# Rows beyond 128 of an expert as float32 strips on unsplit weights, and an earlier gather at expert 0

## The chip, the core and the metric

The kernel runs on one core of a Trainium2 chip. The metric is device time in microseconds (us) of one execution; three runs of the kernel before gave 1434.61 to 1436.72 us, median 1436.69. Engines are named as the profile names them: PE is TensorE's matmul, PEld its weight load, DVE VectorE, ACT ScalarE, POOL GpSimd, SP SyncE, which here issues the loads of weights.

## What is computed

A two-layer model on 512 tokens of width 1024 in float32: one layer of attention with a feed-forward block, one of a short convolution with a mixture of experts. The change is in the mixture: every token goes to 2 of 8 experts, and each expert is a gated block of inner width 1408.

```python
D_MODEL, SEQ, N_EXPERTS, TOP_K, D_FF_EXPERT = 1024, 512, 8, 2, 1408

def moe_swiglu(x, w_router, b_router, w_gate, w_up, w_down):
    ...
    logits = (xt @ w_router).astype(jnp.float32) + b_router.astype(jnp.float32)
    top_logit, top_e = lax.top_k(logits, TOP_K)
    top_w = jax.nn.softmax(top_logit, axis=-1)
    ...
        h = jax.nn.silu(xb @ w_gate[e]) * (xb @ w_up[e])
        return (h @ w_down[e]) * w[:, None].astype(h.dtype)
    ...
    y = jnp.zeros((T, D), x.dtype).at[tok_buf].add(out.reshape(n_rows, D).astype(x.dtype))
```

With the inputs used, the eight experts get 107, 120, 139, 126, 116, 133, 149 and 134 rows (counted from the reference's own inputs): experts 2, 5, 6 and 7 have more than 128.

## The kernel before

Everything ahead of the experts is the same in both kernels and is left aside; in the profiled execution the experts run from 892 us to the end.

**Precision.** A float32 product is made of two parts. `split` writes a number's high part in TensorE's float32r format with ACT (a cast) and the remainder with DVE (a subtraction); `mm3` (lines 502 to 505) then adds three matmuls: high by high, high by low, low by high. This holds for the rows, which are the stationary operand, and for the weights, which stream past.

**Weights.** Class `Weights` keeps one list of all weight chunks in the order of use. A chunk is up to 128 x 1024 float32 (512 KB). `pump` issues a load on SP's queue for the next chunk whenever a raw room is free, and splits a loaded chunk (line 351 on ACT, line 352 on DVE) into a split part whenever a part room is free, up to the number of pieces it is given. A raw room is free again as soon as the chunk is split; a part room when `done` is called for the piece. By `weight_room` there are 6 raw and 3 part rooms in `wb`, 4 and 5 in `wc`, 3 parts in `wa`: 10 raw, 11 parts. Pools `wb` and `wc` are filled in during the layers before; `wc` only begins ahead of expert 0 (line 1662).

**An expert.** `prep` transposes 128 gathered rows into `xgT` (high and low). `gate_up(e, j)` does one of three column groups (512, 512, 384): for u = 0 (gate) and u = 1 (up) 8 steps of `mm3` over the width of 1024, one 512-KB chunk for two steps, 4 chunks for each half. Silu goes to ACT, the product `h` to DVE. `h_transposes` turns `h` into `hT`. `down(e, c)` makes one 512-column half of the output in 11 steps with 6 chunks; the rows are scaled with their share by ACT, and POOL scatters them, adding to the output in DRAM. `done` is called behind each group for all its chunks.

**The rest.** Rows 129 to 192 of an expert (XT = 64) are gathered and transposed as `xe`, high and low side by side as one stationary tile of 128 columns. Behind each group's main matmuls a branch on the expert's row count (`tc.If`, line 1793 in `gate_up`, line 1846 in `down`) runs the block for the rest: per step one matmul of the 128-wide tile on the weights' high part and one of its first 64 columns on their low part (`extra`, lines 1756 to 1761), 32 for the two halves of a group and 22 for a half of down. `both` adds the two lots of 64 result rows (ACT copy at line 1753, DVE addition at line 1754). Down has such a block for each of its halves. A last block (`most > 128 + XT`), which no expert here needs, handles any further rows.

**Order.** The engines run in the order in which the code issues. At expert 0, `first_between` runs between the gate and the up half of the first group: the slot matmuls (line 1685) and the index (line 1687), the gather of the rest's rows (line 1721 on POOL), the shares (lines 1694 to 1704), and the loading of the row counts into registers (line 1710). Then come the up half, the transposes of the rest (line 1745) and the branch.

Of the kernel before, what the change touches and what calls it, by code (L numbers as in the profile page):

```python
# [13 lines left out]
F32 = mybir.dt.float32  # L14
# [24 lines left out]
XT = 64  # L39
# [263 lines left out]
class Weights:  # L303
# [13 lines left out]
    def add(self, src, offset, *shapes):  # L317

        m = sum(k * n for k, n in shapes)
        at = 0  # L320
        for k, n in shapes:
            self.add_part(src, offset, m, at, k, n)
            at += k * n
        return offset + 128 * m

    def add_part(self, src, offset, row, at, k, n):

        self.pieces.append(Piece(len(self.chunks), 0, k, n, True))
        self.chunks.append((bass.AP(tensor=src.tensor, offset=src.offset + offset + at, ap=[[row, 128], [1, k * n]]), k * n))

    def pump(self, pieces=99):

        while True:
# [7 lines left out]
            elif (pieces and self.ready < len(self.pieces) and self.pieces[self.ready].chunk in self.raw  # L341
# [11 lines left out]
                if p.last:  # L353
# [16 lines left out]

    def resume(self, chunks, ahead):
# [7 lines left out]
class Piece:  # L379
    def __init__(self, chunk, at, k, n, last):  # L380
        self.chunk, self.at, self.k, self.n, self.last = chunk, at, k, n, last
# [4 lines left out]
    def lo(self, k, cols=slice(None)):  # L386
        return self.t[:, 1, k * self.n:(k + 1) * self.n][:, cols]

# [28 lines left out]
def kernel(ctx: ExitStack, tc: tile.TileContext, A, out, stop=None):  # L417
# [71 lines left out]
    for e in range(E):  # L489
        off = e * ng  # L490
        for _, n in MOE_GROUPS:
            for a in ("w_eg", "w_eu"):
                W.add(A[a], off, (2, n), (2, n))
                W.add(A[a], off + 128 * 4 * n, (2, n), (2, n))
            off += 128 * 8 * n
        off = e * nd
        for c in range(2):
            for _, n in DN_BLOCKS:
                off = W.add(A["w_ed"], off, (2, 512), (n - 2, 512))
# [1177 lines left out]
    def slots(e):  # L1677
# [10 lines left out]
        yield  # L1688

# [23 lines left out]
    with ExitStack() as l0:  # L1713
# [26 lines left out]
        def extra_prep(e):  # L1740
            xe = mo.tile([128, KD, 2 * XT], F32R, name="xe")
# [4 lines left out]
            split(xe[:, :, :XT], xe[:, :, XT:], pt)  # L1746
            S["e", e] = xe

        def both(dst, p):

            n = dst.shape[1]
            t = mo.tile([XT, 512], F32, name="tb")
            ACT.copy(t[:, :n], p[XT:])  # L1753
            DVE.tensor_tensor(dst, p[:XT], t[:, :n], op=OP.add)

        def extra(p, xh2, wh, wl, start, stop):
            if start:
                PE.matmul(p, xh2, wh, start=True, stop=False)
            PE.matmul(p[:XT], xh2[:, :XT], wl, start=False, stop=False)
            if not start:  # L1760
                PE.matmul(p, xh2, wh, start=False, stop=stop)

        def gate_up(e, j, between=None, after=None):
            c0, n = MOE_GROUPS[j]
            cs = slice(c0, c0 + n)
            if j == 0:
                S["h", e] = mo.tile([128, FE], F32, name="h"), mo.tile([XT, FE], F32, name="he")
                S["hTe", e] = mo.tile([128, NFE, 2 * XT], F32R, name="hTe")
# [3 lines left out]
            ge = mo.tile([XT, 512], F32, name="ge")  # L1772
            ws = [], []
# [221 lines left out]
```

## Time and profile before

| | us |
|---|---|
| median of three runs | 1436.69 |
| lowest and highest run | 1434.61, 1436.72 |
| profiled execution, its own time | 1433.92 |
| its span in the trace | 1432.2 |
| of that, the experts (892.53 to the end) | 539.7 |
| mean granted TensorE clock, of full speed | 0.993 |

The profile is one execution. Its page gives busy time by engine over the whole span; windows of the trace give the same for a stretch; the timeline lists instructions, each with its start, its length, and in brackets how long its engine was idle before it and what ended that. Matmuls are pipelined: the length of one is longer than the time from its start to the next one's start, and it is the latter that adds up. DMA share is the mean busy share of the core's 16 DMA engines. A granted clock of 1.00 is 2.4 GHz, 0.50 is 1.2 GHz.

### The profile page before, as it was taken

The numbers are of one execution on the slowest core, as the hardware profiler recorded it, in microseconds if no ns is written. First come the engines' busy times: TensorE is split into PE (matmuls) and PEld (weight loads), VectorE is DVE, ScalarE is ACT, GpSimd is POOL, SyncE is SP. The second block draws the span as 40 slices with busy tenths as digits, with TensorE's granted clock in tenths as the row PEclk, the third lists the DMA queues.
The fourth block names the chain that finished last, engine by engine and source line by source line (L and its number), as shares of the span: only waits on it lengthen the run. The fifth ranks groups of instructions, "written<-read, shape, count | busy, mean of one in ns | idle before, by whom it ended". The sixth has DMA issues, their size and how long they took to land. (4 is left out here: it accounts for less than half of the span.)

```text
span 1432.2 us, 19340 instructions
## 1 busy us (share of the span) xinstructions
PE 1393.0 (97%) x6956; PEld 1136.0 (79%) x6957; DVE 857.3 (60%) x1391; ACT 700.7 (49%) x1168; POOL 204.4 (14%) x308
## 2 busy tenths in 40 slices
PE   7998999999999999999999999899999999999997
PEld 6866778879888888888988888778788787878785
DVE  4358897855433333434554445899677996666563
ACT  4545896834222221322422223677466775655553
POOL 2258553410000000000000000201102012011100
PEclk9999999999999999999999999999999999999999
DMA  5243001034232232313332224899778997767751
GB/s 190 83 143 122 16 16 60 30 133 148 90 102 89 89 103 74 118 59 118 100 107 94 97 89 167 261 386 378 272 244 282 376 376 269 255 205 245 259 195 24
DMA packets 69416, 231.42 MB, mean 162 GB/s; under 512 B 8752, under 2 KB 10044, under 8 KB 69308
## 3 DMA queue, kind: packets, MB, share of 16 engines
q1 hardware_dynamic: 64332, 217.39, 44.1%
q0 software_dynamic: 3632, 11.06, 3.3%
q10 hardware_dynamic: 1344, 1.58, 0.3%
q8 instruction: 62, 1.02, 0.3%
q14 instruction: 46, 0.38, 0.1%
HBM read 220.53 MB, written 9.47 MB: 161 GB/s over the span
## 5 line engine op out<-in xcount | busy, mean ns | idle before, releaser
L352 DVE TENSOR_TENSOR wbp<-wbr,wbp 128x1024 fp32r<-128x1024 f32 (+2 forms) x104 | 120.9, 1177 | 141.9 <-ACT wbp L351 140.5
L351 ACT CAST wbp<-wbr 128x1024 fp32r<-128x1024 f32 (+2 forms) x104 | 103.8, 1015 | 199.2 <-PE pg L505 108.2
L352 DVE TENSOR_TENSOR wap<-wbr,wap 128x1024 fp32r<-128x1024 f32 (+2 forms) x98 | 113.5, 1173 | 96.0 <-ACT wap L351 94.7
L351 ACT CAST wap<-wbr 128x1024 fp32r<-128x1024 f32 (+2 forms) x98 | 97.8, 1013 | 110.6 <-PE pg L505 73.3
L514 POOL TENSOR_TENSOR rs<-rs,mhalf 128x1 f32<-128x1 f32 x11 | 6.1, 551 | 566.4 <-DVE rs L513 566.4
L352 DVE TENSOR_TENSOR wcp<-wbr,wcp 128x1024 fp32r<-128x1024 f32 (+2 forms) x73 | 80.1, 1128 | 6.0 <-ACT wcp L351 5.0
L1753 ACT COPY tb<-pg 64x512 f32<-64x512 f32 (+1 forms) x32 | 17.8, 556 | 117.5 <-issue 94.8
L351 ACT CAST wcp<-wbr 128x1024 fp32r<-128x1024 f32 (+2 forms) x73 | 68.6, 978 | 9.2 <-PEq L1793 7.7
L503 PE MATMUL pg<-wcp,xgTh 128*128 128x512 f32 (+1 forms) x174 | 66.2, 381 | 0.9 <-PEq L1793 0.2
L505 PE MATMUL pg<-wcp,xgTl 128*128 128x512 f32 (+1 forms) x174 | 65.0, 374 | 0.0
L504 PE MATMUL pg<-wcp,xgTh 128*128 128x512 f32 (+1 forms) x174 | 65.0, 374 | 0.0
L352 DVE TENSOR_TENSOR wcp<-wcr,wcp 128x1024 fp32r<-128x1024 f32 (+2 forms) x57 | 62.5, 1123 | 4.1 <-ACT wcp L351 2.3
L1845 POOL DMA_INDIRECT out_dram<-y,idx x8 | 16.9, 2107 | 291.3 <-ACT y L1840 291.3
L351 ACT CAST wcp<-wcr 128x1024 fp32r<-128x1024 f32 (+2 forms) x57 | 53.6, 972 | 5.0 <-PEq L1793 4.8
L1424 DVE TENSOR_TENSOR x<-pd,x 128x512 f32<-128x512 f32 x48 | 32.3, 688 | 39.2 <-PE pd L505 39.1
L602 POOL TENSOR_TENSOR s<-s,mhalf 128x4 f32<-128x4 f32 (+4 forms) x37 | 35.7, 974 | 69.2 <-DVE s L601 54.7
L1721 POOL DMA_INDIRECT xg<-xd,idx x15 | 20.5, 1364 | 153.5 <-DVE idx L1687 127.9
L626 DVE TENSOR_TENSOR wap<-r,wap 128x1024 fp32r<-128x1024 f32 (+3 forms) x24 | 26.3, 1095 | 26.5 <-ACT wap L623 26.4
L503 PE MATMUL pg<-wbp,xgTh 128*128 128x512 f32 (+1 forms) x104 | 39.4, 379 | 2.3 <-ACT wcp L351 1.7
L503 PE MATMUL pd<-wap,hT 128*128 128x512 f32 x104 | 41.2, 396 | 0.0
L505 PE MATMUL pd<-wap,hT 128*128 128x512 f32 x104 | 41.1, 395 | 0.0
L504 PE MATMUL pd<-wap,hT 128*128 128x512 f32 x104 | 41.1, 395 | 0.0
(561 smaller groups left out, 4235.5 us busy)
## 6 DMA issues: line engine op xcount, KB each, us to landing
wbr<-w_ed SPq DMA_DIRECT2D x48, 512.0 KB, 7.6
wbr<-w_gu SPq DMA_DIRECT2D x44, 512.0 KB, 3.7
wbr<-w_eg SPq DMA_DIRECT2D x40, 512.0 KB, 7.2
wbr<-w_eu SPq DMA_DIRECT2D x40, 512.0 KB, 7.6
wcr<-w_ed SPq DMA_DIRECT2D x32, 512.0 KB, 7.1
wbr<-w_od_in SPq DMA_DIRECT2D x24, 512.0 KB, 3.7
wcr<-w_eg SPq DMA_DIRECT2D x24, 512.0 KB, 7.3
wcr<-w_eu SPq DMA_DIRECT2D x24, 512.0 KB, 7.8
```

The source lines that it names most:

```text
L351: self.nc.scalar.copy(p.t[:, 0, :m], src)
L352: self.nc.vector.tensor_tensor(p.t[:, 1, :m], src, p.t[:, 0, :m].bitcast(F32), op=OP.subtract)
L503: PE.matmul(o, lh, rh, start=start, stop=False)
L504: PE.matmul(o, lh, rl, start=False, stop=False)
L505: PE.matmul(o, ll, rh, start=False, stop=stop)
L514: POOL.tensor_tensor(dst, dst, mhalf[:p, :m], op=OP.pow)
L602: op("POOL", 70 + 78 * n, lambda: POOL.tensor_tensor(rs(), rs(), mhalf[:rs().shape[0], :n], op=OP.pow), (), [buf])
L626: op("DVE", m, lambda: DVE.tensor_tensor(p.t[:, 1, :m], src(), p.t[:, 0, :m].bitcast(F32), op=OP.subtract), [raw], [part])
L1424: DVE.tensor_tensor(x[i][:, cs], ps[c], x[i][:, cs], op=OP.add)
L1721: POOL.indirect_dma_start(out=t, out_offset=None, in_=src, in_offset=rows_of(e, b, n))
L1753: ACT.copy(t[:, :n], p[XT:])
L1845: POOL.indirect_dma_start(out=out, out_offset=rows_of(e, 0), in_=y, in_offset=None, compute_op=OP.add)
```

## The change

XT becomes 32. Rows 129 to 160 of an expert are multiplied in plain float32 on the weights as they were loaded. `xe` and `hTe` hold one float32 copy, 32 columns wide. `strips` puts each 32-column stationary tile on one of four column positions of TensorE's array: step k with operand u goes to result rows 64 (k mod 2) + 32 u, so gate and up of a group (or both halves of down) run in one block, in one PSUM bank, and even and odd steps add up on strips of their own. `halves_of` and one DVE addition join the even and the odd lot; the row's share is multiplied into `he` rather than into `ye`. Down's first half has no branch any more; its second does both halves.

For that, raw chunks are kept (`keep=True`) until `let_go`, behind the group's strips, or behind both halves of down. Split parts are released piece by piece as `mm3` is done with them. The rooms shift: `wc` has 13 raw and 1 part in place of 4 and 5, which makes 19 raw and 7 parts in all. At expert 0, four pieces in place of two are split ahead of the first rows, the second half of the rows is split behind the slots' one-hot rows, and `first_early` runs the slot matmuls and issues the gather behind step 3 of the gate half.

```diff
-XT = 64
+XT = 32
...
-                if p.last:
+                if p.keep:
+                    p.raw, p.raw_slot = self.raw.pop(p.chunk)
+                else:
                     self.raw_free.append(self.raw.pop(p.chunk)[1])
...
+    def let_go(self, *pieces):
+
+        self.raw_free += [p.raw_slot for p in pieces]
+        self.pump(0)
...
+    def whole(self, k):
+        return self.raw[:, k * self.n:(k + 1) * self.n]
...
-    W.pump(2)
-    for b, pt in enumerate(pts):
-        split(first_T[0][:, 4 * b:4 * b + 4], first_T[1][:, 4 * b:4 * b + 4], pt)
-    lx.close()
-    weight_room("wc", 4, 5)
-    W.pump(0)
+    W.pump(4)
+    first_split = lambda b: split(first_T[0][:, 4 * b:4 * b + 4], first_T[1][:, 4 * b:4 * b + 4], pts[b])
+    first_split(0)
...
+    first_slots = slots(0)
+    next(first_slots)
+    first_split(1)
+    lx.close()
+    weight_room("wc", 13, 1)
+    W.pump(1)
...
+        def strips(p, rows, weights):
+
+
+
+            n = len(rows)
+            for k, (x_, pair) in enumerate(zip(rows, weights)):
+                for u, w in enumerate(pair):
+                    o = 64 * (k % 2) + 32 * u
+                    PE.matmul(p[o:o + 32], x_, w, start=k < 2, stop=k >= n - 2)
...
                     mm3(p, xgh[:, k], xgl[:, k], w.hi(k % 2), w.lo(k % 2), k == 0, k == KD - 1)
+                    if k % 2:
+                        W.done(w, splits=0)
                     if k == 3:
+                        if early and u == 0:
+                            early()
                         W.pump(GATE_UP_PACE[2 + u])
...
             with tc.If(regs[e] > 128):
-                for u in range(2):
-                    p = psB.tile([128, 512], F32, name="pg", tag="g")[:, :n]
-                    for k in range(KD):
-                        w = ws[u][k // 2]
-                        extra(p, xe[:, k], w.hi(k % 2), w.lo(k % 2), k == 0, k == KD - 1)
-                    if u == 0:
-                        both(ge[:, :n], p)
-                        ACT.activation(ge[:, :n], ge[:, :n], AF.Silu)
-                    else:
-                        both(he[:, cs], p)
-                        DVE.tensor_tensor(he[:, cs], he[:, cs], ge[:, :n], op=OP.mult)
+                p = psB.tile([128, 512], F32, name="pg", tag="g")[:, :n]
+                strips(p, [xe[:, k] for k in range(KD)],
+                       [[ws[u][k // 2].whole(k % 2) for u in (1, 0)] for k in range(KD)])
+                DVE.tensor_tensor(su[:, :n], p[:64], halves_of(p, n), op=OP.add)
+                ACT.activation(ge[:, :n], su[32:, :n], AF.Silu)
+                DVE.scalar_tensor_tensor(he[:, cs], su[:32, :n], S["w", e, 1][:, e:e + 1], ge[:, :n], op0=OP.mult,
+                                         op1=OP.mult)
...
-            W.done(*ws[0], *ws[1], splits=GATE_UP_PACE[1])
+            W.let_go(*ws[0], *ws[1])
+            W.pump(GATE_UP_PACE[1])
...
+            if c == 0:
+                return
...
+                strips(p, [te[:, f] for f in range(NFE)],
+                       [[both[u][f // 2].whole(f % 2) for u in range(2)] for f in range(NFE)])
...
+        def first_early():
             next(first_slots)
             gather(0, "x", xd, D, ((1, XT),))
-            W.pump(1)
+
+        def first_between():
             shares()
             gather_shares(0)
             load_counts()
```

How the instructions stand on the engines, at three places. First TensorE, the start of a rest's block in expert 0's second group (`xe` is the rest's stationary tile). Names beginning with wa, wb, wc and ending in p are split parts, ending in r raw chunks; `pg` is the result. Before:

```order
L505 MATMUL pg<-wbp_7821,xgTl 128x512
L1793 COMPARE_AND_BRANCH
L1758 MATMUL pg<-wcp_7591,xe 128x512
L1759 MATMUL pg<-wcp_7591,xe 64x512 x2
L1761 MATMUL pg<-wcp_7591,xe 128x512
L1759 MATMUL pg<-wcp_7703,xe 64x512
L1761 MATMUL pg<-wcp_7703,xe 128x512
```
After, from the same place:

```order
L515 MATMUL pg<-wap_7806,xgTl 128x512
L1813 COMPARE_AND_BRANCH
L1770 MATMUL pg<-wcr_7527,xe 32x512
L1770 MATMUL pg<-wcr_7519,xe 32x512
L1770 MATMUL pg<-wcr_7527,xe 32x512
L1770 MATMUL pg<-wcr_7519,xe 32x512
L1770 MATMUL pg<-wcr_7529,xe 32x512
```
The pairs of a wide and a narrow matmul on one split part have become single 32-wide ones that alternate between two raw chunks, up and gate.

Second TensorE again, expert 0's first group, gate half (`pi` is the slot matmuls' result, `oh` the one-hot rows). Before, the last step of the half and what follows it:

```order
L503 MATMUL pg<-wbp_7489,xgTh 128x512
L504 MATMUL pg<-wbp_7489,xgTh 128x512
L505 MATMUL pg<-wbp_7489,xgTl 128x512
L1685 LDWEIGHTS oh
L1685 MATMUL pi<-tok,oh 128x2
L1685 LDWEIGHTS oh
L1685 MATMUL pi<-tok,oh 128x2
```
After, the fourth of the eight steps and what follows it:

```order
L513 MATMUL pg<-wap_7107,xgTh 128x512
L514 MATMUL pg<-wap_7107,xgTh 128x512
L515 MATMUL pg<-wap_7107,xgTl 128x512
L1692 LDWEIGHTS oh
L1692 MATMUL pi<-tok,oh 128x2
L1692 LDWEIGHTS oh
L1692 MATMUL pi<-tok,oh 128x2
```
The slot matmuls have moved from behind 24 matmuls of the half to behind 12.

Third DVE, the same stretch of the program, from the one-hot rows to the index. Before:

```order
L1680 TENSOR_SCALAR oh<-consts,pos 128x256 x4
L352 TENSOR_TENSOR wbp_7528<-wbr_7021,wbp_7528 128x1024
L352 TENSOR_TENSOR wbp_7551<-wbr_7050,wbp_7551 128x1024
L352 TENSOR_TENSOR wcp_7556<-wbr_7079,wcp_7556 128x1024
L352 TENSOR_TENSOR wcp_7574<-wbr_7112,wcp_7574 128x1024
L1687 TENSOR_REDUCE idx<-pi 128x2
L352 TENSOR_TENSOR wcp_7591<-wbr_7487,wcp_7591 128x1024
```
After:

```order
L1687 TENSOR_SCALAR oh<-consts,pos 128x256 x4
L519 TENSOR_TENSOR xgTl<-pt,xgTh 128x512
L352 TENSOR_TENSOR wcp_7541<-wcr_7515,wcp_7541 128x1024
L1694 TENSOR_REDUCE idx<-pi 128x2
L352 TENSOR_TENSOR wap_7578<-wcr_7517,wap_7578 128x1024
L352 TENSOR_TENSOR wap_7581<-wcr_7519,wap_7581 128x1024
L352 TENSOR_TENSOR wap_7597<-wcr_7521,wap_7597 128x1024
```
One weight split instead of four stands between the one-hot rows and the index, beside the split of the rows' second half, which stood ahead of them.

## Rows read from the trace of the kernel before

**Rows 1.** The page: busy us, share of the span, instructions by engine

```profile
PE 1393.0 (97%) x6956; PEld 1136.0 (79%) x6957; DVE 857.3 (60%) x1391; ACT 700.7 (49%) x1168; POOL 204.4 (14%) x308
```

**Rows 2.** Stretches by expert (1, 2, 4, 7): length, busy us, clock, DMA share, GB/s

```profile
950.90:1001.35 50.45, 49.55 (x246) 41.12 (x246) 44.98 (x51) 38.08 (x48) 6.83 (x5) 1.00 1.03 377
1001.35:1081.72 80.37, 80.37 (x396) 64.52 (x397) 53.55 (x64) 45.60 (x62) 9.52 (x6) 1.00 0.77 262
...
1132.11:1182.56 50.45, 49.55 (x246) 41.11 (x246) 45.00 (x51) 38.13 (x48) 6.82 (x5) 1.00 1.02 376
...
1343.34:1432.20 88.86, 78.49 (x373) 62.70 (x371) 44.44 (x51) 41.09 (x56) 4.87 (x3) 0.96 0.45 131
```

**Rows 3.** TensorE's waits in all experts: us in total, times, longest

```profile
PE pt L1745 <- issue: 3.5, 1, 3.5
PE pg L503 <- ACT wcp L351: 1.7, 1, 1.7
PE pd L503 <- PEq L1846: 1.2, 4, 0.3
```

**Rows 4.** Stretches, TensorE alone: expert 2's blocks for its rest, and their sum

```profile
1012.33:1019.64 7.31, 7.31 (x34) 1.00 0.67 262
...
1047.40:1053.04 5.64, 5.64 (x34) 1.00 0.93 337
...
1076.51:1081.72 5.21, 5.21 (x24) 1.00 0.95 289
sum 30.68, PE 30.68; mean PE 6.14
```

**Rows 5.** Timeline, start of such a block: start, us, engine, line, tiles, count

```profile
1012.33 0.39 PE L1758 MATMUL pg<-wcp,xe 128*128 128x512 f32 x1
1012.56 0.62 PE L1759 MATMUL pg<-wcp,xe 128*64 128x512 f32 x2
1013.02 0.39 PE L1761 MATMUL pg<-wcp,xe 128*128 128x512 f32 x1
```

**Rows 6.** Timeline, three runs of float32 passes of 256, 512 and 128 columns

```profile
90.31 1.94 PE L855 MATMUL b<-wap,q 128*64 128x256 f32 x8
...
181.79 1.02 PE L1124 MATMUL b<-x,v 128*128 128x512 f32 x2
...
886.03 6.74 PE L1656 MATMUL pt<-oh,xr 128*128 128x128 f32 x58 [0.43 <-DVE xr L1643]
```

**Rows 7.** Timeline, expert 0's first group; in brackets idle time before and its releaser

```profile
898.07 0.35 PE L1685 MATMUL pi<-tok,oh 128*128 128x2 bf16 x8
...
901.25 0.15 DVE L1687 TENSOR_REDUCE idx<-pi 128x2 int32<-128x4 f32 x1
...
902.30 1.32 POOL L1721 DMA_INDIRECT xg<-xd,idx  x1 [23.53 <-DMA wbr<-w_eu]
...
909.29 0.78 PE L1745 MATMUL pt<-ident,xg 64*128 64x64 f32 x8 [3.45 <-issue]
```

**Rows 8.** Timeline, the last steps behind the last block of expert 7

```profile
1421.91 0.58 ACT L1753 COPY tb<-pg 64x512 f32<-64x512 f32 x1 [4.48 <-PE pg L1761]
...
1423.24 0.72 ACT L1855 ACTIVATE ye<-ye,wg 64x512 f32<-64x512 f32 x1 [0.75 <-DVE ye L1754]
```

**Rows 9.** DMA issues of all experts: count, KB each, median us to landing

```profile
wbr<-w_ed SPq DMA_DIRECT2D x48, 512.0 KB, 7.6
...
xg<-xd,idx POOLq DMA_INDIRECT x15, 9.7
```

**Rows 10.** What SP's load queue waits for in expert 1: us, times, longest

```profile
SPq L338 <- DVE wcp L352: 15.2, 17, 1.7
SPq L338 <- DVE wap L352: 9.6, 9, 3.0
```

**Rows 11.** Stretches, TensorE alone: expert 0's gate half, and behind the idle time

```profile
892.53:898.07 5.54, 5.54 (x28) 1.00 0.99 368
...
910.22:912.92 2.70, 2.70 (x6) 0.50 0.30 100
```

More of the change, by code (lines that the diff above doesn't have):

```diff
@@ L321, in add, with add_part @@
         for k, n in shapes:
-            self.add_part(src, offset, m, at, k, n)
+            self.add_part(src, offset, m, at, k, n, keep)
             at += k * n
         return offset + 128 * m
-    def add_part(self, src, offset, row, at, k, n):
-        self.pieces.append(Piece(len(self.chunks), 0, k, n, True))
+    def add_part(self, src, offset, row, at, k, n, keep=False):
+        self.pieces.append(Piece(len(self.chunks), 0, k, n, keep))
         self.chunks.append((bass.AP(tensor=src.tensor, offset=src.offset + offset + at, ap=[[row, 128], [1, k * n]]), k * n))
@@ L379, with __init__ @@
 class Piece:
-    def __init__(self, chunk, at, k, n, last):
-        self.chunk, self.at, self.k, self.n, self.last = chunk, at, k, n, last
+    def __init__(self, chunk, at, k, n, keep):
+        self.chunk, self.at, self.k, self.n, self.keep = chunk, at, k, n, keep
     def hi(self, k, cols=slice(None)):
@@ L1740, in extra_prep @@
         def extra_prep(e):
-            xe = mo.tile([128, KD, 2 * XT], F32R, name="xe")
+            xe = S["e", e] = mo.tile([128, KD, XT], F32, name="xe")
             g = S.pop(("x", e, 1))
@@ L1745, in extra_prep, with halves_of, gate_up @@
                 PE.transpose(pt[:, k], g[:, k * 128:(k + 1) * 128], ident[:XT, :XT])
[L1746 to L1763, printed above, removed]
+            ACT.copy(xe, pt)
+        def strips(p, rows, weights):
[4 more added lines that the diff above has]
+                    PE.matmul(p[o:o + 32], x_, w, start=k < 2, stop=k >= n - 2)
+        def halves_of(p, n):
+            t = mo.tile([64, 512], F32, name="tb")
+            ACT.copy(t[:, :n], p[64:])
+            return t[:, :n]
+        def gate_up(e, j, between=None, after=None, early=None):
             c0, n = MOE_GROUPS[j]
@@ L1767, in gate_up @@
                 S["h", e] = mo.tile([128, FE], F32, name="h"), mo.tile([XT, FE], F32, name="he")
-                S["hTe", e] = mo.tile([128, NFE, 2 * XT], F32R, name="hTe")
+                S["hTe", e] = mo.tile([128, NFE, XT], F32, name="hTe")
             h, he = S["h", e]
@@ L1772, in gate_up @@
             ge = mo.tile([XT, 512], F32, name="ge")
+            su = mo.tile([64, 512], F32, name="su")
             ws = [], []
@@ L1823, in extra_transposes @@
                 PE.transpose(pt[:, f], he[:, (f0 + f) * 128:(f0 + f + 1) * 128], ident[:XT, :XT])
-            split(t[:, f0:f0 + nf, :XT], t[:, f0:f0 + nf, XT:], pt[:, :nf])
+            ACT.copy(t[:, f0:f0 + nf], pt[:, :nf])
         def down(e, c, between=()):
@@ L1838, in down @@
                     mm3(p, hh[:, f], hl[:, f], ws[-1].hi(f % 2), ws[-1].lo(f % 2), f == 0, f == NFE - 1)
+                    if f % 2 or f == NFE - 1:
+                        W.done(ws[-1], splits=0)
                 if b == 2:
@@ L1843, in down @@
                 W.pump(PACE)
-            if c == 1:
-                POOL.indirect_dma_start(out=out, out_offset=rows_of(e, 0), in_=y, in_offset=None, compute_op=OP.add)
+            if c == 0:
+                return
+            POOL.indirect_dma_start(out=out, out_offset=rows_of(e, 0), in_=y, in_offset=None, compute_op=OP.add)
+            both = S.pop(("d", e))
             with tc.If(regs[e] > 128):
                 te = S["hTe", e]
-                if c == 0:
-                    extra_transposes(e, 8, 3)
+                extra_transposes(e, 8, 3)
                 p = psB.tile([128, 512], F32, name="pg", tag="g")
-                for f in range(NFE):
-                    w = ws[f // 2]
-                    extra(p, te[:, f], w.hi(f % 2), w.lo(f % 2), f == 0, f == NFE - 1)
-                both(ye[:, cs], p)
-                ACT.activation(ye[:, cs], ye[:, cs], AF.Copy, scale=S["w", e, 1][:, e:e + 1])
-                if c == 1:
-                    POOL.indirect_dma_start(out=out, out_offset=rows_of(e, 1, XT), in_=ye, in_offset=None,
-                                            compute_op=OP.add)
-            W.done(*ws, splits=PACE)
+                strips(p, [te[:, f] for f in range(NFE)],
+                       [[both[u][f // 2].whole(f % 2) for u in range(2)] for f in range(NFE)])
+                t = halves_of(p, 512)
+                for u in range(2):
+                    o = slice(32 * u, 32 * u + 32)
+                    DVE.tensor_tensor(ye[:, 512 * u:512 * u + 512], p[o], t[o], op=OP.add)
+                POOL.indirect_dma_start(out=out, out_offset=rows_of(e, 1, XT), in_=ye, in_offset=None,
+                                        compute_op=OP.add)
+            W.let_go(*both[0], *both[1])
+            W.pump(PACE)
         S["T", 0] = first_T
-        first_slots = slots(0)
-        next(first_slots)
-        W.pump(1)
-        def first_between():
+        def first_early():
             next(first_slots)
             gather(0, "x", xd, D, ((1, XT),))
-            W.pump(1)
+        def first_between():
             shares()
@@ L1877 @@
             if e == 0:
[L1878 removed]
+                gate_up(0, 0, first_between, lambda: (extra_prep(0), next(to_come)), first_early)
             else:
```

11 lines of the change are left out of this document (6 added, 5 removed).

## Prediction

> **What bounds the kernel now.** I read the page's share of busy time first: TensorE's 1393 us of a 1432.2 us span, every other engine at 60% or less [rows 1]. Since that is a mean over unlike stages, I then cut the experts' stretch at the first matmul of each expert and read busy time, granted clock and DMA share per expert [rows 2]. The reader should see three things. The clock is at its upper level (2.4 GHz) nearly throughout. An expert with more than 128 rows takes 80.4 us, one without 50.4, and TensorE fills both. DMA is loaded unevenly: share 1.02 to 1.03 in the second of two small experts in a row, 0.77 in a large one. Last I read what TensorE waits for over all eight experts [rows 3]: the largest item is 3.5 us once, at expert 0. So the time here is the sum of TensorE's matmuls, and a matmul removed is time removed as long as weights keep coming.
>
> The four experts that exceed 128 rows are experts 2, 5, 6 and 7. Expert 2's five blocks for its rest, cut at their first and last starts, hold 7.31 us of TensorE twice, 5.64 once and 5.21 twice, with no gap, together 30.68 [rows 4]. The difference 80.37 - 30.68 = 49.7 is a small expert's busy time [rows 2], so these blocks are exposed in full: 4 x 30.68 = 122.7 us.
>
> **The strips.** Before, a block of a 512-column group is 32 matmuls, a 384-column one 32, a half of down 22; one 512-column matmul starts 0.23 us after the one ahead of it whether its stationary tile is 64 or 128 wide [rows 5]. After, gate and up share one block of 16 float32 matmuls and both halves of down one block of 22, each on 32 columns. A float32 matmul is two passes: two 512-column passes take 1.02 us together with 0.59 for one, so one starts 0.43 after the other; eight of 256 columns take 1.94 less 0.43 for the last, over seven, 0.216 each; 58 of 128 take 6.74, or 0.11 each [rows 6]. A 512-column pass is thus 0.427 us and a 384-column one 0.32. The trace has no matmul on any column strip but the first, so how far four strips run side by side is bounded only from both sides: not at all (factor 1) and fully (factor 4).
>
> Fully: a 512 group is 32 passes / 4 x 0.427 = 3.41; a 384 group 8 x 0.32 = 2.56; down has 44 passes, 40 in ten full rounds and 4 in two half-full ones, 12 x 0.427 = 5.12. An expert's rest costs 3.41 + 3.41 + 2.56 + 5.12 = 14.5 instead of 30.68, saving 16.2, or 64.7 over four. Not at all: 32 x 0.427 = 13.65 twice, 10.24, and 18.8, together 56.3, so 4 x 25.6 = 102.5 slower. The factor that breaks even is 56.3 / 30.68 = 1.83. I take 4: the four strips have stationary columns, weights and result rows of their own, neighbours in program order lie on different strips except for the two passes of one matmul, and the queue can hand out matmuls far faster than needed: eight small ones pass in 0.35 us [rows 7], against eight passes per 0.85 us here. What speaks against it is the pair of passes on one strip (first rival). Should each round lose 0.05 us, the 36 rounds of an expert's blocks cost 1.8, or 7 over four; I keep 0 to 7 and take 0.
>
> **Around the strips.** The copy and addition that join the two parts, then Silu and the product, follow a block on ACT and DVE; the same kinds of steps stood there before, DVE is at 53.6 of 80.4 us [rows 2], and TensorE has the next group's first pieces already split. I charge nothing; with that cover gone it would be the chain's own 2.5 us, four steps of 0.58 to 0.72 each [rows 8], at some of 16 blocks. Releasing each split part sooner adds no instruction. The first half of down loses its branch: in each small expert TensorE waits 0.3 us there, 1.2 in four [rows 3]. I take -1.2. At the end, the last block is 5.12 against 5.21, and behind it one copy, two additions and the scatter stand for copy, addition, scaling and scatter [rows 8]: nothing. The transposes of a rest are 32 rows wide instead of 64: eight of the wide ones take 0.78 us [rows 7], and with the eleven behind gate and up at that rate an expert's 19 take 1.9, of which at most half goes: 0 to -3.7 in four. I take 0, since a transpose also has a fixed part.
>
> **Raw weights kept on chip.** Before, a raw chunk's room is free again once DVE has subtracted; after, only behind the whole group, or behind both halves of down. There were 21 rooms of 512 KB, raw and split together, of which a gate group holds 8 and a half of down 6: 13 to 15 ahead. Now 19 raw ones count: 11 ahead in gate groups, 7 at the end of down. TensorE uses a chunk in 6 x 0.228 = 1.37 us, so 7 chunks are 9.6 us of cover; a load lands 7.6 us after its issue [rows 9]. Cheapest is 0: in expert 1, at share 1.03, SP's load queue mostly waits for DVE to free room (15.2 and 9.6 us of 50 in the two largest rows) [rows 10], so the loads were not late. Dearest, one whole landing is exposed in each of experts 1 and 4, where the share is at its top: 2 x 7.6 = 15. I take +1, being nearer to the row that shows loads waiting for room.
>
> **Expert 0's start.** The gate half runs from 892.53 to 898.07 [rows 11]; the eight slot matmuls come only behind it; DVE writes the index at 901.25, behind two splits; POOL issues the gather at 902.30; the transposes of the rest start 7.0 us after that, at 909.29, and TensorE has idled 3.45 us for them [rows 7]. Behind the idle time the clock stands at its lower level, 0.50, for 2.70 us, where 6 matmuls take twice their time: 1.3 us lost [rows 11]. After, the slot matmuls stand behind 12 of the 24 matmuls, at 892.53 + 12 x 0.23 = 895.3, and the index behind one split, near 896.0; the gather then goes out near 896.9. With the 7.0 us it lands at 903.9 and the wait of 3.45 is gone. With the median 9.7 us of these gathers [rows 9] it lands at 906.6, where TensorE would arrive at 909.29 - 3.45 = 905.84, and the gain is 2.7. I take -2.7. The 1.7 us of idle ahead of the up half, which the trace puts to an ACT step [rows 3], I leave: the loading of the row counts still stands at that place. Bounds: 0, if the load queue, at DMA share 0.99 there [rows 11], holds the gather back to its old time, and -6.5, if the wait, the clock and the 1.7 go (3.45 + 1.3 + 1.7).
>
> **Sum.** -64.7 - 1.2 - 2.7 + 1 = -67.6. Against the profiled execution's 1433.9 us that is 1366.3; the median of the runs is 2.8 above that execution, so 1369 as a median. Alone its range is 1361 (head at -6.5, loads at 0, transposes at -3.7) to 1393 (head at 0, loads +15, rounds +7).
>
> **Rivals.** *First: the passes block each other.* In program order each strip's two passes are neighbours, and the second can't run beside the first. If TensorE starts matmuls strictly in order, a pass of strip 0 holds up all that stands behind it: only the second pass of one strip and the first of the next run together. A block of n matmuls then takes n + 1 slots: 17 x 0.427 = 7.26 twice, 17 x 0.32 = 5.44, 23 x 0.427 = 9.81, together 29.8 instead of 30.68. Four experts gain 3.6, and with the other terms -6.5: 1430 (1425 with the head at -6.5 and no late load, 1437 with the head at 0 and loads at +5). The trace speaks neither way: its matmuls start in the order of the program everywhere, but none there stands before a free strip. The Trainium skill, page "TensorE: Matmul & The Clock Gate", Part 3 ("What overlaps and what doesn't"), says that matmuls keep program order in start and in end, which would lead to just this; the trace agrees as far as it goes (starts 0.23 us apart, in order) without a second strip to try it on.
>
> *Second: partial overlap,* a factor near 3.2 by losses at each change of strip: 56.3 / 3.2 = 17.6 per expert, -52.3 for the strips and -55.2 in all, 1381. The same page (closing section, the row on small M) gives 2.38 times for three strips; scaled to four that estimate is 3.17 and about the same time. No run here shows it.
>
> *Third, slower: the strips don't overlap,* because all four take a moving stream that one port delivers. Place: every strip block of the four experts; price +102.5 less the other gains of 2.9, so 1536. It decides as soon as the factor is under 1.83 (1.79 with the other gains). For it speaks that a 64-wide tile costs as much time as a 128-wide one [rows 5]: the stream sets the time, not the columns in use. Against it: eight narrow matmuls pass in 0.35 us [rows 7], so the array takes in several before the first has left it; what each strip's stream needs beside the others no row shows.
>
> *Fourth, slower: loads too late* in experts 1 and 4 while the strips give only the first rival's 3.6: +15 in place of +1, head at 0, so -3.6 - 1.2 + 15 = +10: 1447.
>
> **How the numbers follow.** Full overlap 0.52, first rival 0.27, partial 0.08, no overlap 0.06, fourth or another slower way 0.07. The predicted time is full overlap's, 1369. The range goes from 1361 to 1437, which leaves out the two slower cases and the slowest of the first rival, near 0.18. What can be told from no change is 0.2%, 2.9 us. Faster: 0.52 + 0.08 + 0.17 of the first rival = 0.77; the rest of the first rival splits 0.06 same and 0.04 slower; slower in all 0.17.
>
> **What would show it.** A 512-column strip block: 3.4 us if four run together, 7.3 if two, 13.7 if one; its records in fours with near starts, or in pairs. An expert with a rest at 80.4 - 16.2 = 64.2 us; a small one still 50.4 less 0.3, at experts 1 and 4 above all, else loads are late, and TensorE's waits there name ACT or DVE behind a DMA. At expert 0, the index near 896, the gather near 897, transposes of the rest near 906.6, no stretch at clock 0.50. I'm wrong if the strips start one pass after another, or if TensorE's gaps grow in the experts without a rest.

## The result, and the profile after

The changed kernel takes 1367.81 us (median of four runs, 1366.66 to 1369.74) against 1435.65 for the kernel before beside it: a ratio of 0.9531, with a 95% interval of 0.9513 to 0.9549. Forecast were 1369 us and faster. The profiled execution took 1367.73 us, its span is 1366.0. In a later repeat of the same kernel one execution took 2210.24 us at a granted clock of 0.56, and its median below is of the others.

The page's first section of the kernel after, to be read beside [rows 1]: TensorE is as full as before, over 66 us less.

```profile
PE 1331.1 (97%) x6956; PEld 1061.0 (78%) x6957; DVE 843.9 (62%) x1363; ACT 688.8 (50%) x1144; POOL 206.8 (15%) x308
```

The stretches by expert, cut at the same places as [rows 2] (expert 0 to 2 and 4, all engines, then 5 to 7, TensorE alone; length, busy us and count by engine, clock, DMA share, GB/s):

```profile
891.51:942.99 51.48, 50.76 (x265) 41.82 (x263) 46.30 (x66) 41.91 (x51) 9.17 (x7) 1.00 0.93 349
942.99:994.31 51.32, 49.80 (x246) 41.04 (x246) 44.35 (x50) 38.95 (x48) 8.93 (x5) 1.00 0.98 361
994.31:1059.54 65.23, 65.23 (x396) 46.14 (x396) 51.72 (x58) 44.20 (x59) 9.20 (x6) 1.00 0.83 294
1109.71:1161.84 52.13, 49.83 (x245) 41.04 (x246) 44.69 (x50) 38.92 (x48) 8.17 (x5) 1.00 0.97 356
```

```profile
1161.84:1227.08 65.24, 65.24 (x397) 1.00 0.83 295
1227.08:1292.38 65.30, 65.30 (x399) 1.00 0.81 286
1292.38:1366.00 73.62, 63.72 (x374) 0.95 0.58 196
```

Where the 66.2 us of span went can be added up from these. The four experts with a rest lost 15.1, 15.2, 15.0 and 15.2 us (80.37, 80.48, 80.30 and 88.86 before), together 60.6. Expert 0 lost 6.9 (58.37 before). Experts 1 and 4, the second of two small ones, got longer, by 0.9 and 1.7; expert 3 lost 0.2 (50.39 and 50.17). The part ahead of the experts, where the code is the same, was 1.0 shorter (892.53 and 891.51), which is about what it varies by: in the runs below it ends between 890.4 and 892.8.

TensorE's waits after, answering to [rows 3]. The two waits at expert 0 and the one at down's branch are gone; a new one stands at the transposes of `h`, named after DVE's branch instruction:

```profile
PE pt L1833 <- DVEq L1813: 2.6, 2, 1.7
```

The strip blocks, answering to [rows 4] (expert 2's first 512 group, its 384 group, and down):

```profile
1005.36:1008.93 3.57, 3.57 (x33) 1.00 1.03 415
1033.35:1036.07 2.72, 2.72 (x33) 1.00 1.03 411
1054.27:1059.54 5.27, 5.27 (x46) 1.00 0.49 117
```

And the timeline of the first of these blocks (start, length, line, tiles; `wbr` is up's chunk, `wcr` gate's), answering to [rows 5]:

```profile
1005.36 0.62 PE L1770 MATMUL pg<-wbr,xe 128*32 128x512 f32 x1
1005.37 0.62 PE L1770 MATMUL pg<-wcr,xe 128*32 128x512 f32 x1
1005.38 0.62 PE L1770 MATMUL pg<-wbr,xe 128*32 128x512 f32 x1
1005.38 0.62 PE L1770 MATMUL pg<-wcr,xe 128*32 128x512 f32 x1
1005.82 0.59 PE L1770 MATMUL pg<-wbr,xe 128*32 128x512 f32 x1
...
1006.25 0.59 PE L1770 MATMUL pg<-wbr,xe 128*32 128x512 f32 x1
```

The reader should see starts in fours, 7 ns apart, and one such round every 0.43 us, which is the time of a single 512-column pass in [rows 6]. A float32 matmul by itself shows there as two passes one behind the other. If the passes stand in that order for the strips too, program order would be up, up, gate, gate. The rows go up, gate, up, gate: the first passes of all four strips start before the second pass of the first one. No view here shows the order of the passes in the program; the next experiment shows the same thing on whole matmuls, whose order is that of the code.

### The profile page after: what moved, and what is told of

Its sections match the earlier page's. It is cut to its first block, busy times and chain, and to the rows that moved or that the text cites. A ratio compares the mean times of both kernels' runs of the same rounds, so it can differ in the third digit from the quotient of the medians.

```text
span 1366.0 us, 19153 instructions
## 1 busy us (share of the span) xinstructions
PE 1331.1 (97%) x6956; PEld 1061.0 (78%) x6957; DVE 843.9 (62%) x1363; ACT 688.8 (50%) x1144; POOL 206.8 (15%) x308
## 5 line engine op out<-in xcount | busy, mean ns | idle before, releaser
L352 DVE TENSOR_TENSOR wap<-wbr,wap 128x1024 fp32r<-128x1024 f32 (+1 forms) x88 | 103.5, 1192 | 96.7 <-ACT wap L351 95.4
L351 ACT CAST wap<-wbr 128x1024 fp32r<-128x1024 f32 (+1 forms) x88 | 89.4, 1026 | 113.1 <-PE pg L515 74.1
L352 DVE TENSOR_TENSOR wap<-wcr,wap 128x1024 fp32r<-128x1024 f32 (+2 forms) x84 | 90.8, 1113 | 18.5 <-ACT wap L351 15.8
L352 DVE TENSOR_TENSOR wbp<-wcr,wbp 128x1024 fp32r<-128x1024 f32 (+2 forms) x83 | 91.6, 1127 | 13.1 <-ACT wbp L351 10.6
L351 ACT CAST wap<-wcr 128x1024 fp32r<-128x1024 f32 (+2 forms) x84 | 78.4, 963 | 19.6 <-DMA wcr<-w_eg 10.0
L351 ACT CAST wbp<-wcr 128x1024 fp32r<-128x1024 f32 (+2 forms) x83 | 79.3, 976 | 16.1 <-DMA wcr<-w_eg 5.9
L513 PE MATMUL pg<-wap,xgTh 128*128 128x512 f32 (+1 forms) x168 | 64.1, 382 | 0.7
L513 PE MATMUL pg<-wbp,xgTh 128*128 128x512 f32 (+1 forms) x162 | 61.6, 381 | 1.0 <-PEq L1813 0.2
L515 PE MATMUL pg<-wap,xgTl 128*128 128x512 f32 (+1 forms) x168 | 62.4, 372 | 0.0
L514 PE MATMUL pg<-wap,xgTh 128*128 128x512 f32 (+1 forms) x168 | 62.4, 371 | 0.0
L515 PE MATMUL pg<-wbp,xgTl 128*128 128x512 f32 (+1 forms) x162 | 60.2, 372 | 0.0
L514 PE MATMUL pg<-wbp,xgTh 128*128 128x512 f32 (+1 forms) x162 | 60.2, 372 | 0.0
```

The source lines that it names most:

```text
L351: self.nc.scalar.copy(p.t[:, 0, :m], src)
L352: self.nc.vector.tensor_tensor(p.t[:, 1, :m], src, p.t[:, 0, :m].bitcast(F32), op=OP.subtract)
L513: PE.matmul(o, lh, rh, start=start, stop=False)
L514: PE.matmul(o, lh, rl, start=False, stop=False)
L515: PE.matmul(o, ll, rh, start=False, stop=stop)
```

## Experiments

**The order of the strips.** Three kernels hold the same strip matmuls in other orders. The question was why the two passes of a strip don't hold up the strips behind them, and how far that goes. First, strip by strip:

```diff
-            for k, (x_, pair) in enumerate(zip(rows, weights)):
-                for u, w in enumerate(pair):
-                    o = 64 * (k % 2) + 32 * u
-                    PE.matmul(p[o:o + 32], x_, w, start=k < 2, stop=k >= n - 2)
+            for s in range(4):
+                for k in range(s // 2, n, 2):
+                    PE.matmul(p[32 * s:32 * s + 32], rows[k], weights[k][s % 2], start=k < 2, stop=k >= n - 2)
```

> The same strip matmuls in another order: all of strip 0, then all of strip 32, 64, 96 (4 matmuls, 8 passes, in a row on one strip; in down 5 or 6). The first trace after the change has starts in fours, 7 ns apart, one round per 0.43 us, though in program order a strip's two passes are neighbours. Theory (a pass that waits for its own strip does not hold up those behind it that go to a free one, far enough ahead): a 512 block stays at 3.6 us and the kernel at 1368. Rival (TensorE looks past only a few waiting passes; four strips ran together because the next free strip stood two passes away): the strips take turns, 32 x 0.43 = 13.7 us per 512 block, 10.3 and 18.9 for the others, 56.5 instead of 15.1 per expert, so +165: about 1533. Anything between gives how far it looks.

It took 1458.92 us in one run, in between the 1368 and the 1533 of the two. The three shapes of block, and the start of the first one:

```profile
1005.80:1014.59 8.79, 8.79 (x33) 1.00 1.03 402
1044.23:1050.89 6.66, 6.66 (x33) 1.00 0.28 100
1069.09:1083.03 13.94, 13.94 (x47) 1.00 0.50 110
```

```profile
1005.80 2.33 PE L1769 MATMUL pg<-wbr,xe 128*32 128x512 f32 x5
1007.55 0.62 PE L1769 MATMUL pg<-wcr,xe 128*32 128x512 f32 x1
1007.97 0.59 PE L1769 MATMUL pg<-wbr,xe 128*32 128x512 f32 x1
```

The first row of the timeline holds five passes of strip 0 (2.33 us = 4 x 0.43 + 0.61). The next strip starts at 1007.55, that is 1.75 behind 1005.80, just as the fifth of them starts; three of the eight are then still to come, at 1007.97, 1008.40 and 1008.83, though they stand ahead of strip 1 in the code. So a strip seems to take up to four passes, one running and three waiting, and only a fifth holds up what stands behind it. Played through with 0.429 us a pass this gives 8.6, 6.4 and 13.7 us; with 0.2 for the ends of a block that is the 8.79, 6.66 and 13.94 measured. Neither theory had it: TensorE does look past waiting passes, but not without limit. Two matmuls of a strip in a row are then just allowed:

```diff
+            for k0 in range(0, n, 4):
+                for s in range(4):
+                    for k in range(k0 + s // 2, min(k0 + 4, n), 2):
+                        PE.matmul(p[32 * s:32 * s + 32], rows[k], weights[k][s % 2], start=k < 2, stop=k >= n - 2)
```

> As in the order by strips, but with two matmuls (4 passes) of one strip in a row before the next strip. Theory: unchanged, 3.6 us per 512 block, 1368. Rival, looking past few passes: about half the overlap, 7 us per 512 block, some 30 us per expert and +60: about 1430.

1366.82 us in one run, as the change itself, and blocks nearly as short as the change's:

```profile
1004.70:1008.31 3.61, 3.61 (x34) 1.00 1.02 410
1053.70:1059.00 5.30, 5.30 (x46) 1.00 0.38 76
```

A limit of three passes would have given 4.7 and 5.6 without a block's ends. A limit on the passes that wait in all, whatever their strip, fits no better: here nine wait ahead of the first pass of the last strip, and it starts at 1004.70, 0.05 us behind the block's first at 1004.65, while in the order by strips seven waiting passes held up strip 1. The rule was then put to a forecast, with three matmuls of a strip in a row (`range(0, n, 6)` and `k0 + 6` in the lines above):

> Three matmuls (6 passes) of one strip in a row before the next strip. From the order by strips, where strip 32 began when the fifth pass of strip 0 began, and from pairs, which cost nothing, the theory: passes are handed out in program order, and a strip takes up to four, one running and three waiting; only a fifth holds up those behind it. Played through with 0.429 us a pass, and 0.1 to 0.2 for a block's ends as measured: 6.1 to 6.2 us for a 512 block, 4.6 to 4.7 for 384, 7.0 to 7.1 for down, +36 over four experts: about 1403. Rivals: three per strip would give 7.4 and 10.0, five 4.85 and 5.7.

```profile
1006.31:1012.53 6.22, 6.22 (x34) 1.00 1.02 408
1039.60:1044.32 4.72, 4.72 (x33) 1.00 0.38 141
1062.54:1069.72 7.18, 7.18 (x47) 1.00 0.56 96
```

1404.34 us in one run where 1403 was forecast, and 6.22, 4.72 and 7.18 us for 6.1 to 6.2, 4.6 to 4.7 and 7.0 to 7.1. Four per strip stands; three (7.4 and 10.0) and five (4.85 and 5.7) fall. The blocks account for the whole loss: four experts' blocks are longer than the change's by 92.2 us in the order by strips and by 36.8 in threes, and the kernels are slower by 91.1 and 36.5.

**What a block costs besides its rounds.** Every strip matmul twice:

```diff
+                for v in range(2):
                     for u, w in enumerate(pair):
                         o = 64 * (k % 2) + 32 * u
-                        PE.matmul(p[o:o + 32], x_, w, start=k < 2, stop=k >= n - 2)
+                        PE.matmul(p[o:o + 32], x_, w, start=k < 2 and v == 0, stop=k >= n - 2 and v == 1)
```

> Every strip matmul is issued twice, so the rest's sums are doubled twice over (the output is not the reference's). The blocks were 3.57, 2.72 and 5.27 us where 3.41, 2.56 and 5.12 were forecast, and the main matmuls behind one begin 0.1 late. Theory (a round costs 0.429, and a block has a fixed cost of about 0.15 at its ends): 3.57 + 3.43 = 7.0, 2.72 + 2.57 = 5.3, 5.27 + 5.15 = 10.4 us; four experts +58: about 1426. Rival (the loss belongs to each round): 7.14, 5.44, 10.54, +60.5.

1428.17 us in one run, and a 512-column block and down:

```profile
1007.17:1014.20 7.03, 7.03 (x66) 1.00 1.02 407
...
1065.64:1076.06 10.42, 10.42 (x90) 1.00 0.68 178
```

The 384 block takes 5.32. All three lengths are the theory's and not the rival's. The whole time, 60.4 above the change, is nearer to the rival's 60.5, but the blocks make up only 58.7 of it; the rest lies in experts 1 and 4, which take 52.13 and 53.13 us. 7.03 less 3.57 is 3.46 for eight rounds, 0.43 each, which leaves 0.11 for a block's ends. So the 0.16 by which a block exceeded its forecast of 3.41 is mostly a price of the block, and little of it belongs to its rounds.

**Strips almost gone.** Only the first round of each block is left:

```diff
-            for k, (x_, pair) in enumerate(zip(rows, weights)):
+            for k, (x_, pair) in enumerate(zip(rows[:2], weights)):
...
-                    PE.matmul(p[o:o + 32], x_, w, start=k < 2, stop=k >= n - 2)
+                    PE.matmul(p[o:o + 32], x_, w, start=True, stop=True)
```

> Only the first round of each strip block is left (steps 0 and 1); the others are left out, so the rest's rows are wrong. Theory (the blocks stand wholly on the path): a 512 block 0.86 + 0.15 = 1.0 us, 384 0.8, down 1.0, together 3.8 instead of 15.1 per expert, -45: about 1323. Rival (loads become late as soon as the large experts give less time for them): the waits of 0.9 and 1.7 us that experts 1 and 4 showed come back in every expert behind another, +5 to +15: 1328 to 1338.

1345.15 us in one run: 22.7 less than the changed kernel, where 45 was expected. The block itself is as forecast, but expert 2 takes 57.59 and not 65.23 - 11.3 = 53.9, and expert 3, which has no rest, 53.35 instead of 50.17:

```profile
1004.50:1005.50 1.00, 1.00 (x9) 1.00 1.03 385
```

```profile
993.44:1051.03 57.59, 54.93 (x288) 42.49 (x288) 49.54 (x57) 42.67 (x57) 7.23 (x6) 1.00 0.88 323
1051.03:1104.38 53.35, 50.37 (x249) 40.91 (x246) 45.01 (x52) 38.82 (x48) 10.70 (x6) 1.00 0.96 350
```

The three largest kinds of TensorE's waits in it name DVE, twice with what stands there behind splits of weights (the low half of `h`, and `h` itself) and once with such a split:

```profile
PE pd L515 <- DVE hTl L519: 3.6, 4, 0.9
PE pt L1833 <- DVEq L1813: 3.4, 3, 1.7
PE pg L514 <- DVE wbp L352: 2.3, 3, 0.8
```

So the rival holds, and at a higher price than it named: half of what the missing strips should have freed is given back to weights that come late. The rest's blocks thus seem to be the time in which the loads catch up; no run moves the loads alone to show it. Whether rooms or the rate of the transfers set that limit here was not settled: SP's load queue waits for both.

**Expert 0's gather, back at its old place.**

```diff
-                gate_up(0, 0, first_between, lambda: (extra_prep(0), next(to_come)), first_early)
+                gate_up(0, 0, first_between, lambda: (extra_prep(0), next(to_come)))
...
         def first_between():
+            first_early()
+            W.pump(1)
             shares()
```

> The slot matmuls, the index and the gather of expert 0's rest go back to between the gate and the up half; all else as after the change. By the trace after the change the early gather gave 4.9 us up to the transposes of the rest and 1.3 to 1.4 of clock behind them: +6.3, 1374. By the step of the prediction: +2.7, 1370.5. If another part of the head gave it (the order of splits, four pieces ahead): 0.

1374.2 us, a ratio of 0.9572 (0.9557 to 0.9588): 6.4 slower than the change, where its trace had led to expect 6.3. Index, gather and transposes at expert 0, first of the changed kernel, then of this one with the start of the up half ahead of them, answering to [rows 7]:

```profile
894.73 0.16 DVE L1694 TENSOR_REDUCE idx<-pi 128x2 int32<-128x4 f32 x1
...
895.80 1.32 POOL L1735 DMA_INDIRECT xg<-xd,idx  x1 [18.07 <-DMA wcr<-w_eg]
...
903.35 0.68 PE L1759 MATMUL pt<-ident,xg 32*128 32x32 f32 x8
```

```profile
899.36 0.49 PE L513 MATMUL pg<-wbp,xgTh 128*128 128x512 f32 x1 [0.66 <-issue]
...
901.94 0.15 DVE L1694 TENSOR_REDUCE idx<-pi 128x2 int32<-128x4 f32 x1
...
903.00 1.23 POOL L1735 DMA_INDIRECT xg<-xd,idx  x1 [23.98 <-DMA wcr<-w_eu]
...
908.94 0.65 PE L1759 MATMUL pt<-ident,xg 32*128 32x32 f32 x8 [3.84 <-issue]
```

In the changed kernel the gather goes out at 895.80 and TensorE comes to the transposes at 903.35 without waiting; here it waits 0.66 us ahead of the up half and 3.84 at the transposes, and the clock behind that is at 0.66 for 3.6 us. Expert 0 takes 57.43 us here, 51.48 in the change and 58.37 before. So the earlier gather gives most of the head, 5.95 of 6.9, and the order of the splits around it about 0.9.

**Rooms for raw weights.** The same memory, dealt out as 21 raw and 6 parts (`weight_room("wc", 15, 0)`), or as 17 and 8 (`11, 2`), in place of 19 and 7:

> The same on-chip memory dealt out otherwise: 21 raw rooms and 6 for split parts in place of 19 and 7. Theory (TensorE's waits of 0.9 and 1.7 us in experts 1 and 4 come from raw rooms that come free too late, so that loads are late): both waits go, -2.6: 1365.2. Rival (the DMA rate itself limits there): they stay, 0. Other rival (split parts are short): new waits for ACT or DVE, slower.

1369.9 us, 0.9545 (0.9531 to 0.9559): no difference from the change that can be told. But its experts differ (1 and 2):

```profile
942.77:993.25 50.48, 49.53 (x245) 41.19 (x246) 44.70 (x50) 38.48 (x48) 6.46 (x5) 1.00 0.99 364
993.25:1059.41 66.16, 65.72 (x396) 46.02 (x396) 51.59 (x58) 44.03 (x59) 9.21 (x6) 1.00 0.82 291
```

```profile
PE pg L514 <- DVE wap L352: 1.8, 4, 0.4
```

Experts 1 and 4 are back at 50.48 and 50.43 (51.3 and 52.1 in the change): the two waits came from raw rooms. Experts 2, 5 and 6 are each 0.9 longer, with waits for splits: parts are short there. Expert 7 is not longer. Theory and second rival both hold, and cancel.

> 17 raw rooms and 8 split parts. Theory (rooms limit): two chunks less ahead, each of 1.37 us, in experts 1 and 4 and perhaps at the start of the expert behind them: +3 to +6, 1371 to 1374. Rival (the DMA rate limits): 0.

1384.72 us, 0.9652 (0.9636 to 0.9667): 17 slower, far more than the 3 to 6 expected, and most of it where it was expected: expert 1 takes 57.2, expert 4 55.0, and the large experts behind them 67.0 and 68.1. In expert 1 one wait of SP's load queue is 10.4 us long, for the end of the down block of expert 0, where 12 chunks come free at once; the change has that wait too, at 9.2. New are 8.8 us of waits for the branch behind a group of gate and up (0.9 in the change). Expert 1, then the queue's waits in it, and last that of the change:

```profile
943.40:1000.59 57.19, 52.37 (x246) 42.12 (x246) 44.43 (x50) 39.19 (x48) 8.92 (x5) 0.97 0.91 324
```

```profile
SPq L338 <- PEq L1869: 10.4, 1, 10.4
SPq L338 <- PEq L1813: 8.8, 3, 4.6
```

```profile
SPq L338 <- PEq L1869: 9.2, 1, 9.2
```

**The product ahead of late splits.** In the third group, the two splits issued in the middle of the up half come behind the product:

```diff
-                        W.pump(GATE_UP_PACE[2 + u])
+                        if (j, u) != (2, 1):
+                            W.pump(GATE_UP_PACE[2 + u])
...
                     DVE.tensor_tensor(h[:, cs], p, sg[:, :n], op=OP.mult)
+                    if j == 2:
+                        W.pump(GATE_UP_PACE[2 + u])
```

> In each expert's third group the two splits that are issued in the middle of the up half come behind the product of gate and up on DVE. In experts 1 and 4 TensorE waited 0.9 and 1.7 us for that product, which stood on DVE behind a split whose load was late. Theory (the place in the queue is the cost): the waits go, -2.6: 1365.2. Rival (the late chunk itself is what TensorE needs next): the wait moves to the next main matmul, 0.

1366.86 us, 0.9525 (0.9510 to 0.9539), within the noise of the change. The wait for the product is gone, and 1.2 us of waits for the next split half of `h` stand in its place:

```profile
PE pd L515 <- DVE hTl L519: 1.2, 2, 0.6
```

Half moves, half is gained: experts 1 and 4 take 50.9 and 51.3 in this trace, 102.2 together against 103.45 in the change's.

**One room more.** The sum of the even and odd strips is written over its second summand, which frees 2 KB of each partition; with what was left over that makes room for a twentieth raw chunk:

```diff
-    weight_room("wc", 13, 1)
+    weight_room("wc", 14, 1)
...
-                DVE.tensor_tensor(su[:, :n], p[:64], halves_of(p, n), op=OP.add)
+                su = halves_of(p, n)
+                DVE.tensor_tensor(su, p[:64], su, op=OP.add)
```

> 20 raw rooms and 7 for split parts: the room for one more chunk comes from writing the sum of the even and odd strips into the tile of its second summand. With 21 raw and 6 parts the waits in experts 1 and 4 were gone (50.48 and 50.43 us), but the large experts took 0.93 us more each, from waits for splits. Theory (raw rooms limit experts 1 and 4, parts limit the large ones): experts 1 and 4 near 50.7, the large ones at 65.2, -2 us against the changed kernel. Rival (one room more changes nothing while DMA limits): 0.

> The changed kernel once more, on the same chip as the two before it, so that differences of 0.2% between the three can be read: 0.953 of the kernel before, waits of TensorE in experts 1 and 4 of 0.5 to 1.7 us each.

1364.79 us, 0.9518 (0.9502 to 0.9534), and the changed kernel on the same chip 1367.42, 0.9533 (0.9519 to 0.9547). The intervals overlap, so the gain of 2.6 in the medians is likely and not shown; the profile has it where the theory puts it, experts 1 and 4 at 50.45 and 50.77 against 51.72 and 51.76, the large ones unchanged (65.2 to 65.3 in both):

```profile
941.98:992.43 50.45, 49.84 (x246) 41.09 (x246) 44.37 (x50) 39.05 (x48) 6.92 (x5) 1.00 0.99 366
...
1107.85:1158.62 50.77, 49.84 (x245) 41.09 (x246) 44.31 (x50) 38.96 (x48) 8.91 (x5) 1.00 0.99 364
```

This kernel with 20 raw rooms has the lowest median of those here that leave nothing out.

**Two rooms more, and the product first.** With `weight_room("wc", 15, 1)`, the sum in place and the product ahead of the late splits as above, and the rest's output rows kept in the tile of its inner rows:

> 21 raw rooms and 7 parts, the room from the same sum in place and from keeping the rest's output rows in the tile of its inner rows; and in the third group the splits issued behind the product on DVE. Theory: experts 1 and 4 at 50.4, the large ones at 65.2, -2.6 to -3 us against the changed kernel, 1365. Rival: 0, if the large experts lose by the shared tile (its scatter must have ended before the next expert's rest is written).

1369.93 us, 0.9547 (0.9533 to 0.9560), slower than the change by 2.5 if anything. Experts 1 and 4 are at 50.2 each, as the theory wants, but expert 0 takes 57.0 instead of 51.5. The reason is neither that of the theory nor of the rival. The first load into the pool waits 4.1 us for TensorE's work on the first rows (`pt`), ahead of expert 0, and goes out at 892.26, where the change, without that wait, issues it at 885.88; the larger pool seems to reach into memory that is read up to there. The split ahead of the index then waits for its load, the gather goes out 3.75 us later than in the change, and TensorE waits 2.70 us at the transposes of the rest:

```profile
SPq L338 <- PE pt L1666: 4.1, 1, 4.1
```

```profile
897.35 1.23 DVE L352 TENSOR_TENSOR wcp<-wcr,wcp 128x1024 fp32r<-128x1024 f32 x1 [3.61 <-DMA wcr<-w_eu]
```

```profile
899.55 1.26 POOL L1735 DMA_INDIRECT xg<-xd,idx  x1 [21.44 <-DMA wcr<-w_eg]
```

## Why the prediction was right, and where it was off

**Strips, -64.7 forecast.** The step that decided, a factor of 4, held: 3.57, 2.72 and 5.27 us for 3.41, 2.56 and 5.12, so a rest costs 15.1 us and not 14.5, and the blocks save 4 x (30.68 - 15.13) = 62.2. What the step lacked is the price of a block's ends, 0.11 by the doubled strips, and of the main matmuls behind it: the 24 of a group take 5.57 us there instead of 5.44, some 1.5 to 2 over all blocks, which brings the 62.2 near the 60.6 that the four experts lost. The bound of 0.05 us a round, 7 us in all, was wide enough for these 4 us but laid on the wrong thing: for the most part it is the 16 blocks that cost.

**The first rival** fell by the first timeline: 3.57 and not 7.26. Its premise, that a pass on a busy strip holds up those behind it, is true from the fifth pass of a strip on, as the orders by strip and by threes showed; with two or four in a row it costs next to nothing (3.57 and 3.61 us). The Trainium skill, page "TensorE: Matmul & The Clock Gate", Part 3 ("What overlaps and what doesn't"), has matmuls start strictly in program order; the trace of the order by strips does not agree: strip 1 starts at 1007.55, and three passes of strip 0 that stand ahead of it in the code start later, the first of them at 1007.97. **The second rival**, a factor near 3.2, fell too: 32 passes of 0.427 in 3.57 us are 3.8. The 2.38 times that the Trainium skill's page "TensorE: Matmul & The Clock Gate" ("Why this matters for your kernels", the row on small M) gives for three strips points lower than that, to an estimate of 3.17 for four. **The third** fell with the first; a single strip on its own, in the order by strips, did run one pass per 0.43 us.

**Down's branch, -1.2.** Expert 3, which neither loads nor rests touch, is 0.22 shorter, where 0.3 was forecast.

**Expert 0, -2.7 forecast, 6.6 gained** (6.9 less the branch), just past the far end of the range given, 6.5. The index (forecast near 896.0, less the 1.0 by which the experts began earlier) came at 894.73 and the gather went out at 895.80, as forecast. The term was mis-sized in two things. I priced the landing by the median of all such gathers, 9.7 us, and not by the 7.0 of this very gather in [rows 7]; it landed in time. And I left the idle time of 1.7 us ahead of the up half where it was, while it is gone: TensorE runs through to the transposes, and the loading of the row counts shows in no wait of it. With the slot matmuls back at that place 0.66 of it returned, so that much was theirs and about 1.0 went with the other changes at the head. The clock, which I had only in the bound, stays at 1.00 behind the transposes and is the rest.

**Raw weights kept, +1 forecast.** Two waits of 0.9 and 1.7 us came, in experts 1 and 4, as the rival for them had it and at the size of a small part of a landing. The trace shows the chain in expert 1: ACT waits 1.91 us for a chunk of the down weights, DVE for ACT, the product `h` stands behind that split, and TensorE's transposes behind `h`:

```profile
976.61 1.05 ACT L351 CAST wap<-wcr 128x1024 fp32r<-128x1024 f32 x1 [1.91 <-DMA wcr<-w_ed]
```

```profile
977.69 1.23 DVE L352 TENSOR_TENSOR wap<-wcr,wap 128x1024 fp32r<-128x1024 f32 x1 [1.27 <-ACTq L1813]
978.84 0.55 DVE L1809 TENSOR_TENSOR h<-pg,sg 128x384 f32<-128x384 f32 x1
```

My argument for a low price, that the loads had waited for rooms before, was right about the past and said little on the change: with rooms given back later, the rooms themselves became the limit. How near the edge that is only the runs with 17 and 21 rooms show, at 17 us more for the whole kernel and 2.5 less in those two experts: the dear end of the term, +15, was two rooms away.

**The sum** came out within 2 us because the errors cancel: strips forecast 4 us too good, the head 4 us too poor, loads near 2 us too good, and the start 1.0 us earlier. That closeness is luck; what the prediction had right is the overlap of the four strips and the chain at expert 0.

## What to carry to other kernels

Narrow float32 products belong side by side on column strips, with neighbours in program order on different strips: four 32-column strips ran at 3.8 times the rate of one, on weights that needed no split, and two matmuls of one strip in a row cost next to nothing, three did. Whoever holds a buffer longer to save work has to count the rooms that are left at the tightest stage, not the mean rate of the loads: two rooms fewer cost 17 us here, two more, at the price of one room for split parts, bought 2.5 there and lost as much elsewhere. And where a transfer is made to start sooner, price it by the very transfer in the trace, and look at what stood beside it in the queue.

## What the runs showed of the hardware that I had not expected

A column strip of TensorE takes up to four passes, one running and three waiting, and only the next one holds up matmuls for other strips: shown by three orders (3.61, 6.22 and 8.79 us for the same 32 passes), one of them forecast from the rule to 0.1 us. How the array does this, and whether it holds for other types and widths, no run here shows. Going into and out of strips costs about 0.1 us a block, and the 24 matmuls behind it take 0.13 us more in all, nearly all of it between the first two of them; a like gap stands behind the transposes of `h` (979.75 to 980.06, 0.31 us where 0.23 is usual), so that part is no price of strips alone.
